# A two-layer attention encoder: the queries' projection behind the second half of the values, and the gates' loads behind the last activations of the first run

## The chip, the cores and the metric

The kernel runs on one core of one Trainium2 chip. The metric is the device time of one launch in microseconds (us), as the median of several runs. PE is the matmul engine (TensorE), DVE the vector engine, ACT the scalar engine, POOL GpSimd, SP the engine that issues most loads.

## The reference, cut to what matters

Two layers, each with one combined projection, two groups of attention heads, an output projection, a layer norm, a squared-ReLU MLP and another layer norm. 272 tokens (256 and 16 meta tokens), width 2048, float32.

```python
def _layer(h, w_in, ...):
    proj = jnp.einsum('bld,dp->blp', h, w_in)
    gq, gk, gv, gr, glr, nq, nk, nv = jnp.split(proj, points, axis=-1)   # 512, 512, 1024, 1024, 32, 1024, 1024, 1024
    y_gla = _gla_mixer(gq, gk, gv, gr, glr, gla_w_up, gla_b_up, gla_norm_w)
    y_na = _na_mixer(nq, nk, nv, na_rel_bias).astype(h.dtype)
    mix = jnp.einsum('blm,md->bld', jnp.concatenate([y_gla, y_na], axis=-1), w_out)
    h = _layer_norm(DEEPNORM_ALPHA * h + mix, ln1_w, ln1_b)
    ff = jnp.einsum('blf,fd->bld', jnp.square(jax.nn.relu(jnp.einsum('bld,df->blf', h, w_ff1))), w_ff2)
    return _layer_norm(DEEPNORM_ALPHA * h + ff, ln2_w, ln2_b)
```

In `_gla_mixer` the 32 columns `glr` are multiplied by a small matrix `w_up`; a log-sigmoid of the product gives the decays ("gates") of four heads, in two directions. Queries, keys (512 columns each) and values (1024) enter a gated linear attention, whose result is scaled by a SiLU of the output gate `gr`.

## The kernel before, in words

**Weights.** Every projection is a stream of weight tiles of 128 x 1024 float32 (512 KB). `order` (L154) lists them in the order of use, `made` (L181) loads one into a buffer `raw` and has ACT write its rounded high part `wh` (L212) and DVE the remainder `wl` (L213). `raw`, `wh` and `wl` have three buffers each; `weights` (L175) keeps two tiles made ahead of the one in use. The activations `x` are split into a high and a low part in the same way (L295, L296). A weight tile meets 24 matmuls: high by high, high by low, low by high, over 272 tokens, or over 256 in the second layer where only tokens are needed; there, where the tile is "once", 16 matmuls do (512 columns for high and low together, then 256).

**Two ways to go through a projection.** `by_k` (L258) keeps four results open (eight when `wide`) and takes the weights by rows, so that it can begin while the activations are still arriving. `by_m` (L277) finishes one result of 128 columns after another, two weight tiles each, and hands it to an `evict` function.

**The first run.** In layer 0 the keys and the first half of the values (512 columns) are one wide `by_k` of 16 weight tiles. Before every second tile `load_x` (L381) issues the load of two chunks of x (`xraw`, three buffers) and splits them. The weights' column order in `win` is laid down on the host by `layout` (L1113): keys, first values, queries, second values, output gate, then the other head group.

**Work in between.** Generators sit in two queues, `fg` and `bg`; `pump` (L125) advances them after each half of a result in `by_m`. `gates` (L409) is in `fg`. Its first step in layer 0 issues its three loads (`load_gates`, L401: two of 196 KB and one of 256 KB) and then `consts` (L82): five small loads (`vec`, `ident`, `sel`, `qmask`, `mask`) and some fills and copies on POOL and ACT. `mask` is loaded into a `raw` buffer of the weights and copied by POOL into bytes (L97). The second step splits the 32 gate columns' weights (`ws`, L416), the third prepares `up` (L418 to L424) and issues 32 matmuls (L430), and the next four steps make one head's decays each (L443 to L449: two matmuls, then Abs, Exp, Ln, Exp on ACT). `load_x` takes a step of `fg` at k = 8 and another at k = 12; the remaining ones fall into the `by_m` that follows.

`ev_v` (L458) copies a result of the values to `ft`; after every second one it queues `v_rows` (L465), which transposes the two with six matmuls (L473) and writes them with six ACT and four DVE instructions (L475, L476). The first values' two `v_rows` go to `bg`, the second values' to `fg`, behind `gates`.

**Order around the change** (L346 to L350): the first values are evicted, then come a `by_m` for the queries (eight weight tiles), a `by_m` for the second values (eight), and `drain`, which runs whatever is left in the two queues. Then the output gate begins (L358), and with it `gla_head`, which needs queries, keys and decays, and the values later.

**Queues.** All loads named here are issued by SP, in one order. Their landings are signalled on eight semaphores that the loads take in turn, so a load also waits until the one eight places before it has landed. A build-time scheduler orders each engine's instructions by its own estimate of readiness; engines then run strictly in that order.

Of the kernel before, what the change touches and what calls it, by code (L numbers as in the profile page):

```python
# [7 lines left out]
F32 = mybir.dt.float32  # L8
# [6 lines left out]
P = 128  # L15
D = 2048
DC = D // P
T = 256
NM = 16
L = T + NM  # L20
# [6 lines left out]
WB = 1024  # L27
# [30 lines left out]
class Trunk:  # L58
# [23 lines left out]
    def consts(self):  # L82
        nc, c = self.nc, self.cp
        t = lambda n, s, d=F32: c.tile(s, d, name=n, tag=n)
        t("pad", [P, PAD])
        self.vec = t("vec", [P, DEPTH, 66])
        nc.sync.dma_start(self.vec, self.i["vec"].rearrange("l p v -> p l v"))
        self.ident = t("ident", [P, P])
        nc.sync.dma_start(self.ident, self.i["ident"])
        self.sel = t("sel", [LRK, 2])  # L90
        nc.sync.dma_start(self.sel, self.i["sel"])
        self.qmask = t("qmask", [NM, NK2])
        nc.sync.dma_start(self.qmask, self.i["qmask"])
        self.mask = t("mask", [P, 5, 32], U8)
        raw = self.wp.tile([P, WB], F32, name="raw", tag="raw")[:, :5 * 32].rearrange("p (l c) -> p l c", l=5)
        nc.sync.dma_start(raw, self.i["mask"])
        nc.gpsimd.tensor_copy(self.mask, raw)  # L97
        self.ones = {}
        for n in (GDV, 4 * P, D):
            self.ones[n] = t(f"ones{n}", [P, P])  # L100
            nc.gpsimd.memset(self.ones[n], 1.0 / n)
        self.ones_r = {}
        for n in self.ones:
            self.ones_r[n] = t(f"onesr{n}", [P, P], F32R)
            nc.scalar.copy(self.ones_r[n], self.ones[n])
        self.eps = t("eps", [P, 1])
        nc.gpsimd.memset(self.eps, EPS)
        self.one = t("one", [P, 1])
        nc.gpsimd.memset(self.one, 1.0)
# [44 lines left out]
    def order(self):  # L154

        i, first = self.i, [(), (WB // 2, WB)]
        for l in range(DEPTH):
            last = l + 1 == DEPTH
            na = [last and c % 3 == 0 for c in range(24)]
            groups = [(i["win"][l, g], [last and g in (2, 4, 5)] * 4 if g < 6 else na[4 * g - 24:4 * g - 20]) for g in range(12)]  # L160
            groups += [(i["wout"][l, g], [last and g > 0] * 4) for g in range(4)]
            for half in range(2):
                groups += [(i["wff1"][l, 8 * half + g], [last and (half > 0 or g > 2)] * 4) for g in range(8)]
                groups += [(i["wff2"][l, half, g], [last] * 4) for g in range(4)]
            if l == 0:
                for t in range(groups[0][0].shape[0]):
                    for w, _ in groups[:2]:
                        yield w[t], first.pop(0) if first else (WB,), False
                groups = groups[2:]
            for w, once in groups:  # L170
                n = w.shape[0]
                for t in range(n):
                    yield w[t], (WB,), once[4 * t // n]
# [135 lines left out]
    def layer(self, l):  # L309
        nc, tc = self.nc, self.tc  # L310
        self.l = l
        self.full = l + 1 < DEPTH
        self.n = n = L if self.full else T
        with ExitStack() as actx:
            pool = lambda name, side, ctx=actx, bufs=1: ctx.enter_context(
                tc.tile_pool(name=name, bufs=bufs, side=side, reuse_waits="tile"))
            a = pool("att", "left")
            t = lambda nm, s: a.tile(s, F32, name=nm, tag=nm)
            self.qk = [t(f"qk{h}", [P, 2, L]) for h in range(GH)]
            for h in range(GH) if l else ():  # L320
                nc.gpsimd.memset(self.qk[h][:, 1, T:], 0.0)
            self.decay = [t(f"dec{h}", [P, 2, L]) for h in range(GH)]
            self.V = a.tile([P, 2 * GH, 2, P], F32R, name="V", tag="V")
            self.vlow = [self.pair(self.yp, "y", 12 + h).both.rearrange("p a c -> p (a c)") for h in range(GH)]
            self.VS = a.tile([80, GH * GDV], F32R, name="VS", tag="VS")
            nc.gpsimd.memset(self.VS.bitcast(F32), 0.0)
            self.y, self.gate, self.done, self.vt = [None] * DC, {}, set(), []
            if l:
                self.load_gates()
                self.by_m(self.x, [L + 2] * 4, lambda m, ps: self.fixed(self.ev_k, m, ps), pump=(1, NORMS[0]),  # L330
                          renew=True)
                first = self.by_k(self.x, L, self.normed)
                self.drain()
                self.lctx.close()
            with ExitStack() as ectx:
                self.ep = pool("early", "right", ectx)
                self.fcredit = 0
                self.fg.append(self.gates())
                if l == 0:
                    with ExitStack() as xctx:  # L340
                        self.xr = pool("xr", "right", xctx)
                        first = self.by_k(self.x, L, self.load_x, wide=True)
                    for m in range(4):
                        self.ev_k(m, first.pop(0))
                for m, ps in enumerate(first):
                    self.ev_v(m, ps)  # L346
                self.credit, self.alone = 0, True
                self.by_m(self.x, [n] * 4, self.ev_q, pump=(1, 1, True))
                self.by_m(self.x, [L] * 4, lambda m, ps: self.ev_v(4 + m, ps), pump=(1, 1, True))
                self.drain()  # L350
            self.a2 = pool("na", "left", bufs=2)
            with ExitStack() as gctx:
                self.credit = 0
                self.g2 = pool("gla", "right", gctx, 2)
                for h in range(GH):
                    self.bg.append(self.gla_head(h))
                for g in range(2):
                    self.by_m(self.x, [n] * 4, lambda m, ps: self.ev_r(4 * g + m, ps), pump=(1, GLA_R))  # L358
                self.na_tiles()
                for g in range(6):  # L360
                    if g == 5:
                        while self.bg:
                            self.step(self.bg, 1)
                        gctx.close()
                        self.ln_open()
                    ns = [n if (4 * g + m) % 3 == 0 else L for m in range(4)]
                    self.by_m(self.x, ns, lambda m, ps: self.ev_na(4 * g + m, ps), pump=(1, GLA_NA, True))
            self.alone = False
            ps = self.by_k(self.y, n, self.mixed)
            self.drain()  # L370
        self.tail(ps)
# [9 lines left out]
    def load_x(self, k):  # L381
        if not k:
            self.warm()
            return
        raw = self.xr.tile([P, 2, L], F32, name="xraw", tag="xraw", bufs=3)
        self.nc.sync.dma_start(raw, self.i["xT"][:, k:k + 2, :])
        for c in range(2):
            self.x[k + c] = h, lo = self.pair(self.xp, "x", k + c)
            self.split(raw[:, c, :], h[:, :L], lo[:, :L])
        if k in (8, 12):  # L390
            self.step(self.fg, 1)

    def warm(self):
# [719 lines left out]
def layout(inputs):  # L1113
# [7 lines left out]
    q, k, v, r = w[:, :, 0:512], w[:, :, 512:1024], w[:, :, 1024:2048], w[:, :, 2048:3072]  # L1121
    lr, nq, nk, nv = w[:, :, 3072:3104], w[:, :, 3104:4128], w[:, :, 4128:5152], w[:, :, 5152:6176]
    c = lambda m, j: m[:, :, j * P:j * P + P]
    cols = [k, v[:, :, :512], q, v[:, :, 512:], r] + [c(m, j) for j in range(8) for m in (nq, nk, nv)]

    def tiles(m, kinds, halves=1):

# [15 lines left out]
    w, q = o["win"][0, 0, 0], WB // 4  # L1143
# [19 lines left out]
    p = np.arange(P)  # L1163
# [45 lines left out]
```

## Time and profile before

| What | Value |
|---|---|
| Median of 3 runs | 2341.13 us (2339.74 to 3280.47) |
| The profiled execution's own time | 2342.16 us |
| Its span, first to last instruction | 2340.4 us |
| PE busy in it | 2328.5 us |
| DVE, ACT, POOL busy | 1527.6, 1212.0, 130.9 us |
| Granted TensorE clock | 0.999 |
| Loads | 414.03 MB, 178 GB/s over the span |

PE is busy for 99% of the span, so the time is decided by the matmuls and by the few places where PE waits. In a view, an instruction's row gives its start and its length in us, its engine, its source line, what it writes and reads, how many such instructions follow one another, and in square brackets the idle time of the engine before it with what ended that idle time. Matmuls overlap, so a row's length is more than the time until the next one begins: back to back, 24 of them over 272 tokens take 2.93 us.

### The profile page before, as it was taken

The page shows a single profiled execution, that of the slowest core. Times are in us where ns is not written, and L with a number is a line of the kernel's source. Part 1 is how long each engine was busy: PE and PEld are TensorE (multiplying, and loading weights), DVE is VectorE, ACT ScalarE, POOL GpSimd, SP SyncE. Part 2 cuts the span into 40 slices and gives each one's busy share as a digit, 9 for nine tenths or more (in the row PEclk, how much of TensorE's full clock was granted, in tenths as well). Part 3 has the DMA queues.
Part 4 walks back from the last instruction along what each step waited for, and adds up shares of the span by engine and source line. Part 5 has one row for each costly group of instructions (what it writes and reads, how often), then busy time and mean ns, then how long its engine had stood idle before and what let it go on. Part 6 is the DMA issues. An engine that isn't in the chain of part 4 may idle for free.

```text
span 2340.4 us, 44604 instructions
## 1 busy us (share of the span) xinstructions
PE 2328.5 (99%) x18180; PEld 2215.7 (95%) x18180; DVE 1527.6 (65%) x2432; ACT 1212.0 (52%) x2100; POOL 130.9 (6%) x200
## 2 busy tenths in 40 slices
PE   9999999999999999999999999999999999999998
PEld 9999999999999999999999899999988888888888
DVE  5588777775544455546576787778766555666655
ACT  5666665564433344444456666655644334445443
POOL 0021110110000000000020111100100000000000
PEclk9999999999999999999999999999999999999999
DMA  8455545566656656555555555556666666667664
GB/s 256 153 163 152 161 142 171 172 181 180 180 180 180 181 180 180 180 179 179 178 184 167 168 160 163 158 155 189 194 193 190 191 194 190 191 195 218 192 192 150
DMA packets 118301, 419.02 MB, mean 179 GB/s; under 512 B 13512, under 2 KB 14024, under 8 KB 118096
## 3 DMA queue, kind: packets, MB, share of 16 engines
q1 hardware_dynamic: 117808, 415.65, 58.8%
q8 instruction: 142, 2.33, 0.4%
q14 instruction: 63, 0.52, 0.1%
q10 hardware_dynamic: 288, 0.52, 0.1%
HBM read 414.03 MB, written 2.10 MB: 178 GB/s over the span
## 4 chain that ended last, share of the span: by engine, by line
PE 96%; DVE 2%; ACT 1%; DMA 1%; issue 0%; SPq 0%; DVEq 0%; ACTq 0%
PE mm L247 85%; PE mm L273 6%; PE bg L784 1%; PE bg L273 1%; PE mm L723 1%; DVE wl L213 1%; PE bg L584 1%; PE bg L430 0%; ACT wh L212 0%; DMA xraw<-in_xT 0%; PE mm L749 0%; DVE acc L1012 0%; DMA raw<-in_win 0%; PE bg L635 0%; PE bg L910 0%
## 5 line engine op out<-in xcount | busy, mean ns | idle before, releaser
L213 DVE TENSOR_TENSOR wl<-raw,wh 128x1024 fp32r<-128x1024 f32 (+1 forms) x770 | 942.4, 1225 | 647.8 <-ACT wh L212 640.2
L212 ACT CAST wh<-raw 128x1024 fp32r<-128x1024 f32 (+1 forms) x770 | 804.6, 1046 | 896.1 <-PE mm L247 640.1
L247 PE MATMUL mm<-x,wh 128*128 128x272 f32 (+3 forms) x5376 | 1094.5, 309 | 0.1
L247 PEld LDWEIGHTS mm<-x,wh 128*128 128x128 f32 x5376 | 803.6, 188 | 48.7 <-PE mm L723 0.6
L247 PE MATMUL mm<-x,wl 128*128 128x272 f32 (+3 forms) x3264 | 752.8, 283 | 0.2 <-DVE wl L213 0.2
L247 PEld LDWEIGHTS mm<-x,wl 128*128 128x128 f32 x3264 | 547.4, 188 | 0.6 <-DVE wl L213 0.6
L247 PE MATMUL mm<-y,wh 128*128 128x272 f32 (+2 forms) x2128 | 472.9, 319 | 0.0
L247 PEld LDWEIGHTS mm<-y,wh 128*128 128x128 f32 x2128 | 328.7, 188 | 26.9
L247 PE MATMUL mm<-u,wh 128*128 128x272 f32 (+2 forms) x1552 | 343.7, 318 | 0.0
L247 PE MATMUL mm<-y,wl 128*128 128x272 f32 (+1 forms) x1408 | 337.9, 282 | 0.7 <-DVE wl L213 0.7
L247 PEld LDWEIGHTS mm<-u,wh 128*128 128x128 f32 x1552 | 239.4, 188 | 19.5
L247 PE MATMUL mm<-u,wl 128*128 128x272 f32 (+1 forms) x1024 | 245.6, 282 | 0.0
L247 PEld LDWEIGHTS mm<-y,wl 128*128 128x128 f32 x1408 | 241.7, 188 | 1.4 <-DVE wl L213 1.1
L247 PEld LDWEIGHTS mm<-u,wl 128*128 128x128 f32 x1024 | 175.6, 188 | 0.0
L273 PE MATMUL mm<-x,wh 128*128 128x272 f32 (+1 forms) x512 | 84.4, 287 | 1.5 <-DVE x L296 1.4
L273 PEld LDWEIGHTS mm<-x,wh 128*128 128x128 f32 x512 | 71.5, 189 | 2.3 <-DVE x L296 1.8
L1000 POOL TENSOR_SCALAR acc<-acc,vec 128x272 f32<-128x272 f32 (+1 forms) x24 | 42.0, 1755 | 273.9 <-DVE acc L1012 155.9
L273 PE MATMUL mm<-x,wl 128*128 128x272 f32 (+1 forms) x256 | 51.9, 285 | 0.6 <-DVE wl L213 0.6
L561 ACT COPY U<-S 128x272 f32<-128x272 f32 (+1 forms) x104 | 40.4, 428 | 20.7 <-DVE S L570 19.9
L872 DVE TENSOR_TENSOR acc<-acc,mm 128x256 f32<-128x256 f32 (+1 forms) x71 | 30.2, 425 | 29.3 <-PE mm L247 28.6
L570 DVE TENSOR_TENSOR S<-S,dec 128x272 f32<-128x272 f32 (+1 forms) x112 | 46.7, 446 | 3.7 <-ACT U L561 2.7
L295 ACT CAST u<-ft 128x272 fp32r<-128x272 f32 (+1 forms) x64 | 26.2, 410 | 41.8 <-DVE ft L828 41.7
(265 smaller groups left out, 1649.2 us busy)
## 6 DMA issues: line engine op xcount, KB each, us to landing
raw<-in_wff SPq DMA_DIRECT2D x512, 512.0 KB, 3.7
raw<-in_win SPq DMA_DIRECT2D x190, 512.0 KB, 3.8
raw<-in_wout SPq DMA_DIRECT2D x64, 512.0 KB, 3.7
nb<-in_nab SPq DMA_DIRECT2D x16, 352.0 KB, 4.0
xraw<-in_xT SPq DMA_DIRECT2D x7, 272.0 KB, 5.8
out<-out SPq DMA_DIRECT2D x5, 256.0 KB, 3.1
brow<-in_norm SPq DMA_DIRECT2D x4, 256.0 KB
gw<-in_wup SPq DMA_DIRECT2D x4, 196.0 KB
```

The source lines that it names most:

```text
L212: self.nc.scalar.copy(h, r)
L213: self.wl = self.nc.vector.tensor_tensor(lo, r, h.bitcast(F32), ALU.subtract).ins
L247: mm(o, lhsT=self.block(w, j), rhs=rhs, start=first and not i, stop=last and i == len(TURNS[once]) - 1)
L273: self.nc.tensor.matmul(ps[g + m][:, :n], lhsT=self.block(parts[p][0], 4 * j + m if first else 2 * m + j), rhs=acts[k + j][parts[p][1]][:, ...
L295: self.nc.scalar.copy(hi, src)
L561: nc.scalar.copy(U[:, lv % 4, j, :w].rearrange("p (n t h) -> p n t h", t=2, h=hb), bass.AP(S.tensor, S.offset + 2 * j * L, [S.ap[0], [2 * ...
L570: tt(o, o, totals(lv, odd, w), ALU.mult)
L584: nc.tensor.matmul(ps[b * 32:b * 32 + 32, o:o + w], lhsT=k[:, c:c + 32], rhs=q[:, r:r + w], start=True, stop=True)
L723: nc.tensor.matmul(ps[hh][:, t * NKEY:t * NKEY + NKEY], lhsT=q[hs, NM + t * P:NM + t * P + P], rhs=k[hs, t, :], start=True, stop=True)
L784: nc.tensor.matmul(po[t][hs, :P], lhsT=v2[ts, hs] if rest else v1[:, t, hs], rhs=p2[ts, hh, :] if rest else p1[:, 2 * hh + t, :], start=re ...
L872: tt(a, a, part, ALU.add)
L1000: nc.gpsimd.tensor_scalar(a, a, gain, bias, ALU.mult, ALU.add)
```

## The change

The queries' `by_m` moves behind that of the second values, with the weights' order on the host and the second layer's "once" flags moved to match (the queries' group is now number 3). The first step of `gates`, with its eight loads, moves from k = 8 to k = 14, the last time that activations are loaded; the second step is no longer taken in `load_x` and falls to the first `pump` of the second values. `mask` is staged in an `xraw` buffer in place of one of the weights' `raw` buffers.

```diff
@@ consts
-        raw = self.wp.tile([P, WB], F32, name="raw", tag="raw")[:, :5 * 32].rearrange("p (l c) -> p l c", l=5)
+        raw = self.xr.tile([P, 2, L], F32, name="xraw", tag="xraw", bufs=3)[:, 0, :5 * 32].rearrange("p (l c) -> p l c", l=5)
@@ order
-            groups = [(i["win"][l, g], [last and g in (2, 4, 5)] * 4 if g < 6 else na[4 * g - 24:4 * g - 20]) for g in range(12)]
+            groups = [(i["win"][l, g], [last and g in (3, 4, 5)] * 4 if g < 6 else na[4 * g - 24:4 * g - 20]) for g in range(12)]
@@ layer
                 self.credit, self.alone = 0, True
+                self.by_m(self.x, [L] * 4, lambda m, ps: self.ev_v(4 + m, ps), pump=(1, 1, True))
                 self.by_m(self.x, [n] * 4, self.ev_q, pump=(1, 1, True))
-                self.by_m(self.x, [L] * 4, lambda m, ps: self.ev_v(4 + m, ps), pump=(1, 1, True))
                 self.drain()
@@ load_x
-        if k in (8, 12):
+        if k == DC - 2:
             self.step(self.fg, 1)
@@ layout
-    cols = [k, v[:, :, :512], q, v[:, :, 512:], r] + [c(m, j) for j in range(8) for m in (nq, nk, nv)]
+    cols = [k, v[:, :, :512], v[:, :, 512:], q, r] + [c(m, j) for j in range(8) for m in (nq, nk, nv)]
```

As built, SP's order in the first run changes as follows. Before: x for k = 8, the eight loads of `gates`, weight tiles 10 and 11, x for k = 10, tiles 12 and 13, x for k = 12, tiles 14 and 15, x for k = 14, the first bias tile `nb`, tile 16. After: x for k = 8, tile 10, x for k = 10, tile 11, x for k = 12, x for k = 14, tile 12, the two `w_up` loads, tile 13, the gate columns' weights, tile 14, `vec`, `ident`, `sel`, tile 15, `qmask`, `mask`, `nb`, tile 16. ACT's and DVE's orders follow: ACT's copies of `w_up` (L422) stand right ahead of weight tile 12's cast, and its split of `ws` right ahead of tile 13's. On PE, the 32 gate matmuls stand behind two weight tiles of the second values in layer 0 (behind one of the queries before) and, as before, behind three in layer 1; the second values' transposes stand between the queries' weight tiles in both layers.

## The prediction

> **What bounds the kernel now.** I read the page's busy times first, then PE's waits, then the rows of PE, DVE, ACT and SP around each wait.
>
> ```profile
> span 2340.4 us, 44604 instructions
> PE 2328.5 (99%) x18180; PEld 2215.7 (95%) x18180; DVE 1527.6 (65%) x2432; ACT 1212.0 (52%) x2100; POOL 130.9 (6%) x200
> ...
> PE mm L473 <- ACT ft L460: 1.5, 2, 0.9
> PE mm L273 <- DVE x L296: 1.4, 2, 0.9
> ...
> PE mm L247 <- DVE wl L213: 0.9, 2, 0.7
> ```
>
> PE is busy in all but 11.9 us (2340.4 less 2328.5). The change adds and removes no matmul, so the time can fall only by the waits of PE that it ends, and rise by those that it makes. The second table gives them: us in total, number, longest. Those of L473 (a transpose that waits for ACT's copy `ft`), one of L273's two behind `x`, and one of L247's behind `wl` lie in the stretch that is changed. All others lie elsewhere and stay.
>
> **The first run's wait.** PE's rows, then SP's issues and ACT's copies ahead of it:
>
> ```profile
> 35.21 0.41 PE L273 MATMUL bg<-x,wl 128*128 128x272 f32 x2
> 35.75 0.39 PE L273 MATMUL mm<-x,wh 128*128 128x272 f32 x1
> 37.05 0.74 PE L273 MATMUL mm<-x,wh 128*128 128x272 f32 x3 [0.91 <-DVE x L296]
> ```
> ```profile
> 20.11 0.84 SPq L406 DMA_DIRECT2D gw<-in_wup  x2
> ...
> 23.62 0.33 SPq L93 DMA_DIRECT2D qmask<-in_qmask  x1
> 25.89 0.35 SPq L96 DMA_DIRECT2D raw<-in_mask  x1
> 26.63 3.14 SPq L189 DMA_DIRECT2D raw<-in_win  x2
> 29.82 0.43 SPq L386 DMA_DIRECT2D xraw<-in_xT  x1
> ```
> ```profile
> 20.37 1.23 DVE L213 TENSOR_TENSOR wl<-raw,wh 128x1024 fp32r<-128x1024 f32 x1 [1.14 <-ACT wh L212]
> ...
> 28.19 1.22 DVE L213 TENSOR_TENSOR wl<-raw,wh 128x1024 fp32r<-128x1024 f32 x1 [1.09 <-ACT wh L212]
> ```
> ```profile
> 26.59 0.62 ACT L422 CAST uph<-gw 98x512 fp32r<-98x512 f32 x1
> ...
> 34.33 1.05 ACT L212 CAST wh<-raw 128x1024 fp32r<-128x1024 f32 x1 [3.11 <-DMA raw<-in_win]
> ```
> ```profile
> 19.64 6.19 DMA xraw<-in_xT
> ```
>
> A tile of 24 matmuls takes 2.93 us, 0.12 each. Tile 11 should have begun 0.24 after 35.21, at 35.45; it began at 35.75, and its second matmul came at 37.05 where 35.87 was due: 0.30 and 1.18, together 1.48 us lost. It waited for `wh` (the cast at 34.33 had waited 3.11 for its load) and then for the x of k = 10, whose load SP issued only at 29.82. SP was late because of the gates' eight loads: it stood from 23.95 (23.62 and 0.33) to 25.89, until the x chunk issued eight loads earlier had landed (19.64 and 6.19 is 25.83), and issued tile 10 at 26.63, when ACT, too, could take up the first gate load (26.59).
>
> **The two drains and the gates' crowd in layer 1.**
>
> ```profile
> 108.98 0.49 PE L473 MATMUL mm<-ident,ft 128*128 128x128 f32 x3
> ...
> 110.36 0.55 PE L473 MATMUL mm<-ident,ft 128*128 128x128 f32 x3 [0.60 <-ACT ft L460]
> 110.67 0.74 PE L247 MATMUL mm<-x,wh 128*128 128x272 f32 x4
> ...
> 1290.39 0.82 PE L473 MATMUL mm<-ident,ft 128*128 128x128 f32 x6
> 1290.97 0.74 PE L247 MATMUL mm<-x,wh 128*128 128x272 f32 x4
> ...
> 1299.91 0.49 PE L473 MATMUL mm<-ident,ft 128*128 128x128 f32 x3
> 1301.29 0.55 PE L473 MATMUL mm<-ident,ft 128*128 128x128 f32 x3 [0.89 <-ACT ft L460]
> 1301.59 0.48 PE L247 MATMUL mm<-x,wh 128*128 128x512 f32 x1
> ```
> ```profile
> 1274.12 0.28 PE L247 MATMUL mm<-x,wl 128*128 128x256 f32 x1
> 1274.46 0.77 PE L247 MATMUL mm<-x,wh 128*128 128x272 f32 x4
> 1275.16 0.33 PE L584 MATMUL bg<-qk 128*32 128x32 f32 x16
> 1275.72 0.52 PE L247 MATMUL mm<-x,wl 128*128 128x272 f32 x2 [0.23 <-DVE wl L213]
> ```
>
> Six transposes cost 0.58 when nothing is awaited (1290.39 to 1290.97). After the last second values PE takes 1.68 from the transposes to the next weights in layer 1 (1299.91 to 1301.59): 1.10 lost. In layer 0 it takes 1.69 (108.98 to 110.67), in which small matmuls of the next stage also stand; the idle time says 0.60, and 1.69 less 0.58 and some 0.36 of those matmuls is 0.75. At 1274 tile 409, the first of the second values, starts 0.22 late (1274.46 against 1274.24) and loses 0.4 more before `wl` comes (1275.72, behind small matmuls that filled part of the hole): about 0.65, since ACT was behind with the gates.
>
> **The change part by part.**
>
> *Gates' first step to k = 14, `mask` out of `raw`.* Tile 10's load no longer stands behind the eight loads; it needs tile 7's `raw`, which DVE frees at 21.60 (20.37 and 1.23), so it is issued 5.0 earlier than 26.63. The x of k = 10 follows at about 22.0 in place of 29.82; even with 6.19 to land it is there at 28.2, against 35.45. Tile 11 needs tile 8's buffer and comes some 5 earlier too. The 1.48 go. What is late next are the gates' own loads, as ACT copies them ahead of the casts of tiles 12 and 13:
>
> ```profile
> gw<-in_wlr SPq DMA_DIRECT2D x1, 256.0 KB, 6.8
> raw<-in_win SPq DMA_DIRECT2D x3, 512.0 KB, 4.3
> ```
>
> The two `w_up` loads go out behind tile 12's, which waits for tile 9's `raw`. DVE freed that at 29.41 (28.19 and 1.22), about 0.5 of it due to the gate copy that ACT made ahead of the cast (26.59); so 28.9, and the loads by 30.1. Landing takes 4.3 to 6.8: 34.4 to 36.9. A copy of 0.62 and a cast of 1.05 end tile 12's `wh` at 36.1 to 38.6. PE wants it at 38.38 (35.45 and 2.93): from 2.3 ahead to 0.2 late. Tile 13, behind `wlr`, has about the same margin, one tile later on both sides. I take 0.2 lost: the first run gains 1.28, between nothing (all the 1.48 moved to tile 12) and 1.48. POOL's mask copy, `vec`, `ident` and the fills cost nothing: POOL is busy for 6%, and the transposes that need `ident` begin only behind the second values' first result. `nb` and tile 16 have as many bytes ahead of them as before. The Trainium skill, DMA: Bandwidth & Descriptors, Rules for kernel authors, tells one to issue a DMA early and wait for it late, which speaks against this step: by it the gates' loads, issued 9 us later than now, should surface as a wait. No row here shows that yet; by that rule the first run would gain nothing.
>
> *Queries behind the second values.* Both drains go, as the transposes then stand between the queries' tiles, whole tiles after their `ft` was copied: 0.75 and 1.10. If that cover failed they would cost the same again at the end of the queries, where nothing but the queries' eviction is left. The gates now share ACT with the second values:
>
> ```profile
> L446 ACT ACTIVATE gt<-gt,one 128x544 f32<-128x544 f32 x4 | 3.0, 753 | 0.0
> L444 ACT ACTIVATE gt<-bg 128x272 f32<-128x272 f32 x8 | 2.7, 397 | 0.0
> L449 ACT ACTIVATE dec<-gt 128x544 f32<-128x544 f32 x4 | 2.7, 673 | 0.0
> L445 ACT ACTIVATE gt<-gt 128x544 f32<-128x544 f32 x4 | 2.6, 661 | 0.0
> ...
> L453 ACT ACTIVATE qk<-jn 128x256 f32<-128x256 f32 x3 | 1.2, 409 | 0.0
> L254 ACT COPY jn<-mm 128x256 f32<-128x256 f32 x3 | 1.1, 368 | 0.0
> ```
>
> A head costs ACT 2.75 (11.0 over 4), nearly a whole weight tile's 2.93, beside its cast of 1.05: ACT falls behind for four tiles. In layer 1 a query costs it 0.78 (0.41 and 0.37), a value one copy of about 0.4, and a value's tile runs longer on PE (24 matmuls of 272 for 16): 1.2 less work over three results, and more time. The 0.65 go. In layer 0 a query is one copy already, but the gates start one weight tile later:
>
> ```profile
> 82.64 1.23 DVE L213 TENSOR_TENSOR wl<-raw,wh 128x1024 fp32r<-128x1024 f32 x1 [0.80 <-ACT wh L212]
> ...
> 85.28 0.41 PE L247 MATMUL mm<-x,wl 128*128 128x272 f32 x2
> ```
>
> The tile that follows the gates has its `wl` at 83.87 and uses it at 85.28, 1.41 ahead. A shift by one tile, 2.93, would make it 1.5 late if nothing else moved; but in the new order ACT makes the previous cast earlier and has no query to evict at that place, which I put at the rest. I take 0.15 lost, between 0 and 1.5. *Flags, column order:* the tiles and matmuls are the same, no cost.
>
> **The sum.** 1.28 + 0.75 + 1.10 + 0.65 - 0.15 = 3.6 us off the profiled execution's 2342.16 (span 2340.4 and 1.76 around it). That execution is 1.0 above the median of the runs, 2341.13; off the median it gives 2337.5.
>
> **Rivals.**
> A, forecast: all four waits go, 2337.5 (2336.2 to 2338.8).
> B: the first run's wait only moves, to tiles 12 and 13 behind the gates' copies on ACT; 2.3 remain, 2338.8. For it: the 6.8 of `wlr`, above. Against it: tile loads land in 4.3. By the Trainium skill's rule named above this is what should happen.
> C: the crowd on ACT makes a wait of up to 1.5 in layer 0's second values, 2338.9; if layer 1's stays too, 2339.5.
> D, slower: ACT, strictly in order, stands before the gates' `w_up` and `wlr` with the casts of tiles 12 and 13 behind it, and PE with it. Each us that they land after 36.7 (38.38 less 0.62 and 1.05) is lost. It decides from 3.8 lost, at 40.5: 10 us or more from issue to landing, where the longest row here is 6.8. At 12 the time is 2343.
> E: the drains stay because ACT's `ft` copies are late again at their new place; 1.85 less, 2339.4. Against it: weight tiles stand between.
>
> **How the numbers follow.** A 0.55, B 0.17, C 0.14, D 0.06, E 0.05, the rest 0.03. The time is A's, 2337.5. The runs themselves spread (2339.74, 2341.13, and 2342.16 profiled), about 1.2 either way. A's lower end 2336.2 less 1.0 for that gives 2335.2; at the top B, C and E (to 2339.5) and the spread, 1.2, give 2340.7, and D is left out: 2335.2 to 2340.7. A measurement of this kernel can tell about 2%, 47 us, from no change; no case reaches it, so within 2% has 0.98, either side 0.01 for what I have not seen.
>
> **What would show it.** Right: no wait of L273 near 36 us, no L473 behind `ft`, L247 behind `wl` down to 0.2; PE's busy time the same and the span 3 to 4 us shorter. Wrong: PE waiting for `wh` or `wl` at 38 to 42 (B, D), near 83 (C), or for `ft` among the queries (E); a stage far from the change moving by more than 1 us would be something I have not reckoned with.

## The result and the profile after

The changed kernel takes 2336.59 us (median of 22 runs, 2335.85 to 2338.08), the kernel before 2341.18 (22 runs; the one of 3280.47 stands apart from all others and does not enter the ratio). The ratio is 0.998, with a 95% interval of 0.9974 to 0.9986: 4.6 us or 0.2% less, between 3.3 and 6.1. The prediction said 2337.5 and 3.6 less.

Profile page of the changed kernel: the span and the busy times, then the table of PE's waits (engine, operation, line and what it waited for: us in total, number, longest).

```profile
span 2334.9 us, 44618 instructions
PE 2326.3 (100%) x18180; PEld 2216.0 (95%) x18180; DVE 1527.4 (65%) x2432; ACT 1211.8 (52%) x2100; POOL 129.4 (6%) x200
```
```profile
PE bg L399 <- DVE zero L396: 1.2, 1, 1.2
PE mm L247 <- DVE wl L213: 0.7, 1, 0.7
PE mm L273 <- DVE wl L213: 0.5, 1, 0.5
PE bg L910 <- ACT sp L295: 0.2, 1, 0.2
```

PE's 18180 instructions are the same. The transposes' wait for `ft`, the waits for `x` and the shorter of L247's two waits for `wl` are gone, and no wait has come that was not there. The two profiled executions lie 5.4 apart (2340.4 and 2334.9), more than the medians.

Where the 5.4 came from, by the start of the same weight tile on PE in the two traces: 1.7 at tile 11 of the first run, 0.85 over layer 0's queries and second values, 2.4 over the same in layer 1, 0.2 near 1245 us, and 0.3 that was there before tile 11. That last piece is not the change: the execution of before waits 0.47 for `x` at 17.69, the one of after does not, though nothing is moved up to there.

The first run in the changed kernel, SP's issues, ACT's work and PE:

```profile
21.68 0.33 SPq L189 DMA_DIRECT2D raw<-in_win  x1
22.06 0.42 SPq L386 DMA_DIRECT2D xraw<-in_xT  x1
23.59 0.33 SPq L189 DMA_DIRECT2D raw<-in_win  x1
```
```profile
33.15 0.62 ACT L422 CAST uph<-gw 98x512 fp32r<-98x512 f32 x1 [0.81 <-DMA gw<-in_wup]
34.25 0.62 ACT L422 CAST uph<-gw 98x512 fp32r<-98x512 f32 x1 [0.48 <-DMA gw<-in_wup]
34.78 1.04 ACT L212 CAST wh<-raw 128x1024 fp32r<-128x1024 f32 x1
```
```profile
35.11 0.65 PE L273 MATMUL mm<-x,wh 128*128 128x272 f32 x4
...
38.04 0.65 PE L273 MATMUL bg<-x,wh 128*128 128x272 f32 x4
```

Tile 10 is issued at 21.68, the x of k = 10 at 22.06, tile 11 at 23.59, and PE goes from tile 10 into tile 11 (35.11) and on to tile 12 (38.04, 2.93 later) without a hole. ACT did stand for the gates' loads (0.81 and 0.48 of idle time), in front of tile 12's cast, which ended at 35.82 (34.78 and 1.04), 2.22 ahead of PE.

Layer 0: the queries' first tile, right behind the second values and the gates, then the end of the queries; PE, and DVE's subtraction for that first tile:

```profile
83.35 0.75 PE L247 MATMUL mm<-x,wh 128*128 128x272 f32 x4
83.94 0.41 PE L247 MATMUL mm<-x,wl 128*128 128x272 f32 x2
...
107.44 0.41 PE L247 MATMUL mm<-x,wl 128*128 128x272 f32 x2
107.68 0.65 PE L247 MATMUL mm<-x,wh 128*128 128x272 f32 x4
```
```profile
82.23 1.22 DVE L213 TENSOR_TENSOR wl<-raw,wh 128x1024 fp32r<-128x1024 f32 x1 [0.35 <-ACT wh L212]
```

The tile that starts at 83.35 had its `wl` at 83.45 (82.23 and 1.22) and used it at 83.94, 0.49 ahead, where the same margin was 1.41 before: close, but no wait. At 107.68 the output gate's tiles begin straight behind the queries.

Layer 1, the same places:

```profile
1274.93 0.82 PE L473 MATMUL mm<-ident,ft 128*128 128x128 f32 x6
1275.50 0.48 PE L247 MATMUL mm<-x,wh 128*128 128x512 f32 x1
...
1284.07 0.82 PE L473 MATMUL mm<-ident,ft 128*128 128x128 f32 x6
1284.65 0.48 PE L247 MATMUL mm<-x,wh 128*128 128x512 f32 x1
```

The six transposes cost 0.57 and 0.58 between the queries' tiles, and no bracket stands in these rows.

### The profile page after: what moved, and what is told of

Its sections match the earlier page's. It is cut to its first block, busy times and chain, and to the rows that moved or that the text cites. A ratio compares the mean times of both kernels' runs of the same rounds, so it can differ in the third digit from the quotient of the medians.

```text
span 2334.9 us, 44618 instructions
## 1 busy us (share of the span) xinstructions
PE 2326.3 (100%) x18180; PEld 2216.0 (95%) x18180; DVE 1527.4 (65%) x2432; ACT 1211.8 (52%) x2100; POOL 129.4 (6%) x200
## 4 chain that ended last, share of the span: by engine, by line
PE 98%; DVE 1%; issue 0%; ACT 0%; DVEq 0%; ACTq 0%
PE mm L247 86%; PE mm L273 6%; PE bg L273 1%; PE bg L784 1%; PE mm L723 1%; PE bg L584 1%; DVE wl L213 0%; PE bg L430 0%; PE mm L749 0%; DVE acc L1012 0%; PE mm L473 0%; PE bg L635 0%; PE bg L910 0%; PE bg L665 0%; PE bg L639 0%
## 5 line engine op out<-in xcount | busy, mean ns | idle before, releaser
L247 PE MATMUL mm<-x,wh 128*128 128x272 f32 (+3 forms) x5376 | 1094.3, 309 | 0.0
L247 PEld LDWEIGHTS mm<-x,wh 128*128 128x128 f32 x5376 | 803.7, 188 | 48.1 <-PE mm L723 0.6
L247 PE MATMUL mm<-x,wl 128*128 128x272 f32 (+3 forms) x3264 | 752.7, 283 | 0.0
L247 PEld LDWEIGHTS mm<-x,wl 128*128 128x128 f32 x3264 | 547.5, 188 | 0.0
L247 PE MATMUL mm<-y,wh 128*128 128x272 f32 (+2 forms) x2128 | 472.9, 319 | 0.0
L247 PEld LDWEIGHTS mm<-y,wh 128*128 128x128 f32 x2128 | 328.6, 188 | 26.9
L247 PE MATMUL mm<-u,wh 128*128 128x272 f32 (+2 forms) x1552 | 343.7, 318 | 0.0
L247 PE MATMUL mm<-y,wl 128*128 128x272 f32 (+1 forms) x1408 | 337.9, 282 | 0.7 <-DVE wl L213 0.7
L247 PEld LDWEIGHTS mm<-u,wh 128*128 128x128 f32 x1552 | 239.4, 188 | 19.5
L247 PE MATMUL mm<-u,wl 128*128 128x272 f32 (+1 forms) x1024 | 245.6, 282 | 0.0
L247 PEld LDWEIGHTS mm<-y,wl 128*128 128x128 f32 x1408 | 241.7, 188 | 1.4 <-DVE wl L213 1.1
L247 PEld LDWEIGHTS mm<-u,wl 128*128 128x128 f32 x1024 | 175.6, 188 | 0.0
```

What stands on the lines that cost most here:

```text
L247: mm(o, lhsT=self.block(w, j), rhs=rhs, start=first and not i, stop=last and i == len(TURNS[once]) - 1)
```

## The experiments

Two theories stood for the first run's wait. The prediction's: SP stood behind the gates' eight loads, so tile 10's load and the x behind it were late. The rival: it is the staging of `mask` in a weights' buffer alone. The three `raw` buffers are handed out in turn, so `mask` pushes every later tile one place on: tile 10 takes tile 8's buffer in place of tile 7's, and tile 11 has to wait for tile 9's in place of tile 8's. For the two layers' part the question was the size, and how much of it is the drains and how much the crowd on ACT. Of the drains alone no kernel was made.

**1. The loads' part alone** (before, with the step at k = 14 and `mask` out of `raw`).

```diff
-        raw = self.wp.tile([P, WB], F32, name="raw", tag="raw")[:, :5 * 32].rearrange("p (l c) -> p l c", l=5)
+        raw = self.xr.tile([P, 2, L], F32, name="xraw", tag="xraw", bufs=3)[:, 0, :5 * 32].rearrange("p (l c) -> p l c", l=5)
...
-        if k in (8, 12):
+        if k == DC - 2:
```

> The gates' loads move to the last activations and the mask leaves the weights' buffer, but the queries stay ahead of the second values. Theory (four separate waits of PE, each ended by its own edit): the wait behind x near 36 us goes, the two waits for ft at the drains (0.6 and 0.9) and the crowd at the end of layer 1's queries stay; the traces of before and after put the first wait at 1.7 us, so 2341.2 - 1.7 = 2339.5. Rival (the first run's difference is only how the two executions happened to start, and all the gain is the reordering's): 2341.2, no change.

Measured: 2339.98 us, ratio 0.9992 (0.9983 to 1.0001) to the runs of before beside it (2342.03); span 2338.2. The wait near 36 us is gone. The drains' two waits (1.5 in all) and L247's two (0.9 in all) stand in the table of waits as they did before the change.

The loads' part gives 2.2 us between the spans, 1.7 of it at tile 11. The interval of the ratio reaches 1.0 here and in runs 3, 4 and 5, so the medians alone do not show this part; it is read from the traces. Since `mask` is moved too, the run does not tell the two theories apart.

**2. The order alone** (the changed kernel with the gates' steps back at k = 8 and 12 and `mask` back in `raw`).

```diff
-        if k == DC - 2:
+        if k in (8, 12):
...
-        raw = self.xr.tile([P, 2, L], F32, name="xraw", tag="xraw", bufs=3)[:, 0, :5 * 32].rearrange("p (l c) -> p l c", l=5)
+        raw = self.wp.tile([P, WB], F32, name="raw", tag="raw")[:, :5 * 32].rearrange("p (l c) -> p l c", l=5)
```

> The queries move behind the second values; gates' loads and mask stay where they were. Theory: the wait behind x near 36 us stays (about 0.9 in the table of waits, 1.7 with the restart), both waits for ft go and the crowd of layer 1 goes; by the two traces 0.8 in layer 0 and 2.4 in layer 1, so 2341.2 - 3.2 = 2338.0. Rival (the loads' move carries the gain, the drains' waits come back at the end of the queries): under 1.5 gained, 2339.7 or more, with PE waiting for ft or wl near 109 or 1300.

Measured: 2338.21, ratio 0.9985 (0.9977 to 0.9994); span 2336.5. PE at the first run's place:

```profile
36.56 0.75 PE L273 MATMUL mm<-x,wh 128*128 128x272 f32 x3 [0.91 <-DVE x L296]
```

The wait of 0.91 behind `x` stays as it was; the drains are gone. From tile to tile layer 0 gives 0.95 and layer 1 2.4. The two parts add up about: 2.2 and 3.9 us of span, each with an execution's own spread in it, against 5.4 for both.

**3. `mask` alone** (before, with the one line of the staging buffer changed as in 1; SP's order is as before).

> Before, with one line changed: the mask is staged in a buffer of the activations and not in one of the weights' three. Theory (SP is held by the eight loads ahead of weight tile 10 and by their landings): SP's order is as before, tile 10's load still goes out after 26 us, the wait near 36 us stays at 1 us or more, 2341. Rival (the mask held one of three weight buffers, and that alone delayed the weights): tile 10's load goes out some 4 us earlier, no wait near 36 us, 2339.5.

Measured: 2339.77, ratio 0.9991 (0.9982 to 1.0); span 2337.8. SP's issues, ahead of which stand the same eight loads of the gates, then DVE's end of tile 9 and PE at tile 11:

```profile
24.89 0.35 SPq L96 DMA_DIRECT2D xraw<-in_mask  x1
25.63 0.82 SPq L189 DMA_DIRECT2D raw<-in_win  x2
26.64 0.33 SPq L386 DMA_DIRECT2D xraw<-in_xT  x1
```
```profile
27.19 1.22 DVE L213 TENSOR_TENSOR wl<-raw,wh 128x1024 fp32r<-128x1024 f32 x1 [1.05 <-ACT wh L212]
```
```profile
34.84 0.41 PE L273 MATMUL mm<-x,wl 128*128 128x272 f32 x2
35.08 0.65 PE L273 MATMUL mm<-x,wh 128*128 128x272 f32 x4
```

For comparison, the chain of waits in before, over the same stretch (start, length, what):

```profile
28.19 1.24 DVE wl L213
...
29.45 0.33 SPq L189
...
29.82 0.43 SPq L386
```

In before, SP issues tile 11 at 29.45, in the moment when DVE has finished tile 9 (28.19 and 1.24 is 29.43); the x of k = 10 stands behind it, and on ACT and DVE its split stands behind tile 11's cast and subtraction as well. With `mask` elsewhere, tiles 10 and 11 and the x go out together at 25.63 to 26.64, before DVE has even begun tile 9's subtraction (27.19), and PE does not wait. The eight loads still stand ahead of tile 10, which goes out 1.0 earlier than before and not 5; so by themselves they do not make PE wait, and the place in the ring is needed for the wait. So far the rival holds.

That the loads had no part in the wait of before is not shown. They take most of the room: tile 10 has its `wl` 0.30 before PE wants it here, and 1.71 in the changed kernel. And tile 9's subtraction, which tile 11 has to await in before, ends there at 29.43 and in the changed kernel at 27.24: ACT casts tile 9 in before only behind the split of the x that landed at 25.83 and the copy of the first gate load (26.59). A kernel with `mask` in `raw` at k = 8 and the other seven loads moved was not made.

**4. The eight loads split** (before, `mask` out of `raw`, the gates' three loads at k = 8 and the five of `consts` at k = 14).

```diff
-        if k in (8, 12):
+        if k in (8, DC - 2):
...
         self.load_gates()
+            yield
```

> Before, with the gates' three loads (0.67 MB) still at k = 8, but the five constants (0.22 MB, five of the eight loads) at k = 14 and the mask out of the weights' buffer. Theory (number of loads, since they share eight landing signals and SP issues in order): weight tile 10's load goes out near 22 us in place of 26.6, the wait near 36 us falls under 0.5; time about 2339.8. Rival (bytes: three quarters of them still stand ahead of the weights): the wait stays at three quarters of 1.7, that is 1.2, time 2341. The gates' second step falls to the queries, one weight tile later than before, which may cost up to 0.5 near 84 us in either case.

Measured: 2339.58, ratio 0.9993 (0.9983 to 1.0002); span 2337.9, and no wait near 36 us. Beside run 3 it says nothing more: `mask` is out of `raw` here too, and every kernel of that kind loses the wait.

**5. The loads moved, `mask` left in `raw`** (before, with the step at k = 14 alone, the second edit of 1).

> Before, with the first gate step moved to k = 14, but the mask still staged in one of the weights' three buffers. Mask theory (of e3: the mask's place in the ring of weight buffers makes tile 11's load wait for tile 9's buffer instead of tile 8's): the ring is clear near 36 us, so that wait of 1.7 goes, and the mask now stands between weight tiles 15 and 16: tiles 16 to 18 are issued a buffer, up to 2.9 us, later, which eats their margins of 2.6 to 4.5 us and may leave a wait of up to 1 near 50 to 58 us. Time 2340.0. Loads theory (of the prediction: the eight loads hold SP): the same as e1, no wait anywhere in the first run.

Measured: 2339.92, ratio 0.9996 (0.9987 to 1.0005) against 2340.70 beside it; span 2337.8. The wait near 36 us is gone here as well, and none came where `mask` is now staged; an execution's own 0.36 near 11 us is there. This speaks neither for the first theory nor against it, since `mask` moves along with the loads. What the pushed ring costs shows at its new place: tile 16 has its cast 1.41 ahead of PE, against 2.56 in the changed kernel.

**6. The order and `mask`, with the loads left where they were** (the changed kernel with the first edit of 2).

> The changed kernel with the gates' steps put back to k = 8 and k = 12: queries behind second values and the mask out of the weights' buffers, nothing else. Mask theory: nothing is lost against the changed kernel, no wait of PE near 36 us, and the gates again start one weight tile earlier; 2336.6, within 1 of it. Loads theory: the wait near 36 us is back by 1 us or more; 2338.0.

Measured: 2336.53 (2335.45 to 2337.37, 11 runs), ratio 0.9981 (0.9972 to 0.999); span 2335.0. PE's waits are the changed kernel's four, and one more, near 17 us, before the places in question:

```profile
PE mm L273 <- DVE x L296: 0.2, 1, 0.2
```

That is the changed kernel's ratio, 0.998 (0.9974 to 0.9986), without the move of the loads. Beside the other two edits the move brings nothing that the medians can tell. In the trace it is worth a little: tile 11 takes 3.23 here (35.05 to 38.28) where 2.93 is due, a loss of 0.30 in gaps too short for the table. Its first matmuls, and the subtraction for the x of k = 10, which runs until 35.50:

```profile
35.05 0.90 PE L273 MATMUL mm<-x,wh 128*128 128x272 f32 x4
```
```profile
34.71 0.79 DVE L296 TENSOR_TENSOR x<-xraw,x 128x272 fp32r<-128x272 f32 x2
```

**7. `mask` staged twice through `raw`** (before, with the three staging lines run two times; lines further down are one higher).

```diff
-        raw = self.wp.tile(...)
-        nc.sync.dma_start(raw, self.i["mask"])
-        nc.gpsimd.tensor_copy(self.mask, raw)
+        for _ in range(2):
+            raw = self.wp.tile(...)
+            nc.sync.dma_start(raw, self.i["mask"])
+            nc.gpsimd.tensor_copy(self.mask, raw)
```

> Before, with the mask loaded twice, each time through one of the weights' buffers (80 KB more). Mask theory: a second of the three weight buffers is taken, tile 10's load now waits for tile 9's buffer (free at 29.4), lands near 33.5 and is cast by 34.6, where PE wants it at 32.5; PE waits 2 to 3 us there and about as long again behind it, 3 to 6 us in the first run in place of 1.7. Loads theory: one more small load, 0.3 us more on SP, the wait of 1.7 grows by 0.5 at most.

Measured: 2346.11 (one run); span 2344.3. SP, DVE and PE:

```profile
26.73 1.03 SPq L97 DMA_DIRECT2D raw<-in_mask  x2
30.23 0.80 SPq L190 DMA_DIRECT2D raw<-in_win  x2
```
```profile
28.98 1.23 DVE L214 TENSOR_TENSOR wl<-raw,wh 128x1024 fp32r<-128x1024 f32 x1 [1.04 <-ACT wh L213]
```
```profile
32.60 0.42 PE L274 MATMUL mm<-x,wl 128*128 128x272 f32 x2
36.23 0.77 PE L274 MATMUL bg<-x,wh 128*128 128x272 f32 x4 [3.21 <-ACT wh L213]
37.49 0.82 PE L274 MATMUL bg<-x,wl 128*128 128x272 f32 x2 [0.49 <-DVE wl L214]
```

Pushed by two places, tile 10 itself needs tile 9's buffer: it goes out at 30.23, as DVE ends at 30.21 (28.98 and 1.23), and PE waits 3.21 and 0.49 for tile 10. By its bytes a second load of `mask`, 80 KB, is 0.3 us at the 262 GB/s of the first run.

From tile 9's start to tile 13's PE takes 11.73 in the changed kernel and in runs 1, 3, 4, 5 and 9, 13.44 in before and 17.91 here: one place cost 1.7, two cost 6.2. Not all of the 6.2 is waiting. Behind the long wait the clock that PE is granted is half of the full one, as this window shows (its bounds and length in us, then busy us of PE, of its weight loads PEld, of DVE, ACT and POOL with the number of instructions, granted clock, DMA share, GB/s):

```profile
38.00:40.00 2.00, 2.00 (x11) 2.00 (x10) 2.00 (x4) 1.11 (x2) 0.00 (x0) 0.50 0.74 207
```

From 37.49 to tile 11's start at 41.48 the last 20 matmuls of tile 10 take 3.99 where 2.44 is due, so about 1.5 of the 6.2 came with the slower clock. Behind the wait of 0.91 in before the granted clock stayed at 1.00.

Runs 3, 6 and 7 together show that, with the eight loads standing where they stood, the place in the ring decides whether PE loses more than the 0.30 of run 6. How much the loads add to the wait stays open.

**8. The queries of layer 1 in the longer form** (before, where they take 24 matmuls of 256 columns, with ACT's copy `jn` and the addition gone, since the result comes in one part).

```diff
-            groups = [(i["win"][l, g], [last and g in (2, 4, 5)] * 4 if g < 6 else na[4 * g - 24:4 * g - 20]) for g in range(12)]
+            groups = [(i["win"][l, g], [last and g in (4, 5)] * 4 if g < 6 else na[4 * g - 24:4 * g - 20]) for g in range(12)]
...
-                self.by_m(self.x, [n] * 4, self.ev_q, pump=(1, 1, True))
+                self.by_m(self.x, [n] * 4, self.ev_q, pump=(1, 1, True), slim=range(4))
```

> Before, with the second layer's queries taken as 24 matmuls of 256 columns for each weight tile in place of 16, so that ACT copies a query once (0.4) and not twice (0.8) and PE needs no less time. Crowd theory (ACT's surplus of work beside the gates made what PE lost at the end of layer 1's queries; by the two traces 1.2 us at tiles 409 and 410, where the prediction read 0.65): the lost time there falls under 0.5, while the drain's wait for ft (0.9) stays. Rival (the loss belongs to the change from one kind of tile to the other, or to the gates' chain itself): it stays at about 1.

Measured: 2344.08 (one run); span 2342.3. PE from the gate matmuls over the end of the queries to the drain, and in before the same gate matmuls:

```profile
1253.76 4.15 PE L430 MATMUL bg<-x,ws 128*64 128x272 f32 x32
...
1274.35 0.67 PE L247 MATMUL mm<-x,wh 128*128 128x272 f32 x4
1274.85 0.41 PE L247 MATMUL mm<-x,wl 128*128 128x272 f32 x2
...
1289.08 0.82 PE L473 MATMUL mm<-ident,ft 128*128 128x128 f32 x6
...
1299.01 0.33 PE L584 MATMUL bg<-qk 128*32 128x32 f32 x16
1299.98 0.33 PE L473 MATMUL mm<-ident,ft 128*128 128x128 f32 x1 [0.63 <-ACT ft L460]
```
```profile
1253.81 4.15 PE L430 MATMUL bg<-x,ws 128*64 128x272 f32 x32
```

The loss at the end of the queries is gone, and the drain's wait stays (0.63 behind 16 small matmuls that fill part of it, against 0.89). From the 32 gate matmuls to the last transposes ahead of the drain, PE takes 35.32 here (1253.76 to 1289.08) and 36.58 in before (1253.81 to 1290.39): 1.26 less. In it, the 16 small matmuls of L584 that ran in the hole of before come later (0.15 less), and five tiles in the longer form take about as much more. So the crowd cost about 1.3. The run takes away the change from one kind of tile to the other at this place as well, so by itself it does not exclude that rival. The trace of before speaks for the crowd: ACT shows no idle time there from 1261.41 to 1279.16, and in that stretch stands tile 409's cast, which ends at 1274.41 where PE was due to begin at 1274.24:

```profile
1273.36 1.05 ACT L212 CAST wh<-raw 128x1024 fp32r<-128x1024 f32 x1
```

Later the kernel of run 8 loses more than it won. PE waits 1.86 at L910 near 1339 us (0.2 in before), and the granted clock then stands at 0.50 to 0.51 from 1341 to 1344 us:

```profile
1342.00:1343.00 1.00, 1.00 (x5) 0.90 (x5) 1.00 (x2) 0.78 (x2) 0.00 (x0) 0.50 0.07 29
```

Why that wait grew was not looked into, so the total is no verdict on this form.

**9. More loads at the moved place** (the changed kernel with 1 MB that nothing reads, ahead of the gates' loads).

```diff
+            for c in range(4):
+                fat = self.yp.tile([P, 2, PITCH], F32, name=f"fat{c}", tag=f"y{c}", bufs=1).rearrange("p a c -> p (a c)")[:, :512]
+                nc.sync.dma_start(fat, self.i["wff1"][1, 0, c, :, :512])
```

> The changed kernel with four added loads of 256 KB each (1 MB of weights that nothing reads) ahead of the gates' eight loads, at the same place, step 14 of the first run. It asks how much room the moved loads have: in the changed kernel tile 16, the first whose load stands behind them on SP, is cast 2.56 us and has its remainder 1.80 us before TensorE wants it. View that only bytes count: 1 MB at the 262 GB/s that the first run moves is 4.0 us, tile 16's load lands that much later, so TensorE waits for tile 16 some 1.5 to 2.5 us near 50 us, and the span is 2336.5 to 2337.5. View that the first run's loads don't fill the DMA engines there (tiles 10 to 13 keep 2 us and more of room): tile 16 loses under 1.8 us of its margin, no wait shows, and the span is 2334.5 to 2336. In both views the waits of layer 1 and the drains stay as in the changed kernel.

Measured: 2336.52 (one run); span 2334.7, with no new wait. The window of 30 to 40 us, first the changed kernel's, then this one's, and ACT's copies of `w_up` here:

```profile
30.00:40.00 10.00, 10.00 (x84) 10.00 (x83) 6.33 (x9) 7.15 (x11) 0.00 (x0) 1.00 0.86 260
```
```profile
30.00:40.00 10.00, 10.00 (x84) 10.00 (x83) 5.11 (x7) 4.09 (x7) 0.00 (x0) 1.00 0.92 315
```
```profile
40.28 0.62 ACT L425 CAST uph<-gw 98x512 fp32r<-98x512 f32 x1 [3.96 <-DMA gw<-in_wup]
...
42.47 0.62 ACT L425 CAST uph<-gw 98x512 fp32r<-98x512 f32 x1 [0.62 <-DMA gw<-in_wup]
```

In this window 315 GB/s were moved where 260 had been, which is 0.55 MB more in 10 us, about half of the added 1 MB; of the rest, some shows from 50 to 60 us (255 GB/s against 214). Tile 16 has its cast 2.26 ahead of PE in place of 2.56: it lost 0.3 and not the 4 us of the bytes. The gates' copies on ACT came 7 to 8 us later (40.28 and 42.47 against 33.15 and 34.25), now ahead of the casts of tiles 14 and 15. The first stood 3.96 for its load; still tile 14's cast ended 2.0 and tile 15's 2.1 before PE wanted them, where the changed kernel has 4.2 for both.

## Why the prediction was right, and where its working was wrong

The time was right, 2337.5 against 2336.59, inside the range; case A is what happened: all four waits went, and none came. One of its causes does not suffice, and most of its sizes were too low. By its own steps:

*The first run.* The new places were right: tile 10 at 21.6 and the x at 22.0 were expected, 21.68 and 22.06 came. The size was near: 1.28 was taken, 1.7 came. The 0.2 set aside for tiles 12 and 13 was not lost, and 0.2 was lost in before that the prediction did not count, behind the wait: three matmuls took 0.58 from 37.05 on, where 0.37 is due.

```profile
37.63 0.41 PE L273 MATMUL mm<-x,wl 128*128 128x272 f32 x2
```

The cause that the prediction gave does not suffice. "SP was late because of the gates' eight loads": with the loads in place and `mask` out of the ring nothing was lost in run 3 and 0.30 in run 6, and with the same loads and one more place in the ring 6.2 was lost (run 7). The term came true by luck in this, that the change takes `mask` out of the ring in the same step; a kernel that moved the loads and left `mask` at its old place in the order is not among the runs. The prediction did read that tile 10 needs tile 7's `raw` in the changed kernel; but it put tile 11's lateness into one heap with tile 10's, and did not ask why SP's row at 26.63, two issues, was 3.14 long. Two issues without a wait took 0.82 in run 3: the rest was tile 11's wait for a buffer.

*The gates' loads late (B).* ACT did stand for them, 0.81 and 0.48, and in run 9 even 3.96; PE waited in neither, with tile 12's cast 2.22 ahead (2.3 ahead to 0.2 late was expected). The advice of the Trainium skill, DMA: Bandwidth & Descriptors, Rules for kernel authors, to issue a DMA early and wait for it late, was weighed against the step. The trace shows the later issue (27.64 against 20.11 for the first of the gates' loads), but not the loss on PE that was read from the rule. That the median does not need the move either (run 6) is a finding of the runs, not of the rule.

*D, ACT in order.* Its place was right (ACT's order does put the copies ahead of the casts of tiles 12 and 13) and its price was not reached. In run 9 the second copy, at 42.47, is past the 40.5 from which D was to decide, but there the copies stand two tiles further on in ACT's order, presumably because the build-time scheduler reckoned with the added loads. A load that is later than the scheduler reckoned, which is what D needs, was not made.

*Drains.* Right: layer 1's 1.10 went wholly, as the six transposes take 0.58 in their new place. Layer 0's 0.75 is not told apart from the rest of what layer 0 gave. E did not happen.

*The crowd in layer 1.* Right in kind, too small: 0.65 taken, about 1.3 found (2.4 over the stage less 1.10; 1.3 in run 8). The prediction added 0.22 and about 0.4 of tile 409 and stopped. The starts of tiles 410 and 411 in before, and `wl` late once more inside tile 410:

```profile
1278.32 0.65 PE L247 MATMUL mm<-x,wh 128*128 128x272 f32 x4
1278.98 0.52 PE L247 MATMUL mm<-x,wl 128*128 128x272 f32 x2
...
1281.58 0.66 PE L247 MATMUL mm<-x,wh 128*128 128x272 f32 x4
```

Tile 409 takes 3.86 (1274.46 to 1278.32) and tile 410 3.26, where 2.93 is due: 0.22, 0.93 and 0.33 are 1.48, less 0.15 for the 16 small matmuls that ran inside the hole and now run later.

*The new crowd in layer 0 (C).* 0.15 was set aside; no wait came, and layer 0 gave 0.85, where 0.75 less 0.15 was forecast. The margin fell from 1.41 to 0.49, so the concern was a fair one; a shift by a whole tile did not come.

*The signs.* Two were misread. PE's busy time did not stay the same: it fell from 2328.5 to 2326.3, so 2.2 of the 5.4 lie in matmuls that take longer around a wait and count as busy (the first run lost 1.7 and shows 0.91 of idle time). And L247 behind `wl` did not fall to 0.2: the wait that went is the shorter one, 0.23 at 1275.72, and the one of 0.7, which lies behind 1400 us, stays.

*The balance.* 1.7, 0.85 and 2.4 are 5.0 in the profiled pair, against the predicted 3.6. The median moved 4.6, between 3.3 and 6.1; either sum lies in that interval, so the sizes above are read from the traces, not from the medians. Over the traces they repeat: from the first of the 16 tiles of queries and second values to the output gate, layer 1 takes 56.25 to 56.36 in the six kernels with the old order (run 8 apart) and 53.91 or 53.92 in the four with the new one; layer 0, from tile 13 to tile 33, 67.60 to 67.68 and 66.57 to 66.71.

## What to carry to other kernels

Where buffers are handed out in turn, a small thing staged in the main stream's ring costs no bytes worth naming but pushes each later tile by one buffer; look for a load that is issued in the moment when an engine frees a buffer, and count which tile's buffer that is. Before a late issue is blamed on the loads ahead of it, move the cheapest suspect alone: here one line gave what the move of eight loads was credited with (run 3's 2339.77 beside run 1's 2339.98). And a stall that starts at one tile is summed until the tiles are back at their even pace, not to the end of the bracket that names it.

## What was not expected of the hardware

A long wait of PE cost more than its own length: behind 3.21 (run 7) and 1.86 (run 8) the granted clock was 0.50 for some 3 us, behind 0.91 (before) it stayed at 1.00. What between these lengths decides, no run tells.

Loads at a place that was already at 0.86 of the DMA engines' time could be added to without a wait on PE: from 260 to 315 GB/s in 30 to 40 us.

Executions differ in the first 20 us, over a stretch in which all these kernels are the same: a wait of 0.47 behind `x` near 17 us is in the profiled execution of before and not in that of after, a wait of 0.36 near 11 us in run 5 alone. With an effect of 4.6 us this alone is a tenth, which is why the stages were compared from tile to tile.
